# High and low weight parts for two feature pairs at a time, and a shorter bank-by-bank end

## The chip, the cores and the metric

The kernel runs on one core of one Trainium2 chip. The metric is the device time of one execution in microseconds (us). TensorE (PE) multiplies, VectorE (DVE), ScalarE (ACT) and GpSimd (POOL) work on elements, and SyncE (SP) issues most of the transfers.

## The reference

One layer of a hybrid block over 512 tokens and 2048 features, in float32:

```python
h = rmsnorm(x, norm1_w[l])
proj = jnp.einsum('bsd,de->bse', h, w_in[l])          # 2048 -> 22592 columns
q, k, v, g_ret, z, xbc, dt_raw, gate_r, gate_s = jnp.split(proj, offsets, axis=-1)
y_r = retention(q, k, v, positions) * silu(g_ret)     # 8 heads x 256
y_s = ssd(xbc, dt_raw, conv_w[l], ...)                # 64 heads x 64
y_s = rmsnorm(y_s * silu(z), ssd_norm_w[l])
p_r = jnp.einsum('bse,ed->bsd', y_r, w_br_ret[l])     # 2048 x 2048
p_s = jnp.einsum('bse,ed->bsd', y_s, w_br_ssd[l])     # 4096 x 2048
merged = sigmoid(gate_r) * p_r + sigmoid(gate_s) * p_s
x = x + jnp.einsum('bsd,de->bse', merged, w_out[l])   # 2048 x 2048
return rmsnorm(x, norm_f_w)
```

Nearly all of the work is the five products with weights. The rest, retention and the state-space scan, is done between them.

## The kernel before

**Tiling.** Every product with weights is cut into units of 256 output columns by 512 tokens over 2048 features. The features of a unit are taken in eight feature pairs (`NP`), each 256 rows of the weights. A unit either uses seven products per feature pair (`SEVEN`, Strassen's products in Winograd's form, four PSUM banks, on seven weight forms of 128 columns) or eight plain ones (`EIGHT`, three banks, four weight forms). The trace holds 101 units of the first kind; the others, and the two passes of the last unit, are plain.

**Parts.** A float32 operand is split into a high part, rounded to the type that TensorE takes at speed, and a low part, which is the remainder. ACT copies to the high part and DVE subtracts (`split`, lines 150 and 151). Each product is then three matmuls: weight high by activation high (line 202), weight high by activation low (line 203), weight low by activation high (line 204). `hh` and `hl` are the parts of the activations, eight tiles of each for a whole stage; `whi` and `wlo` are those of the weights.

**The weight pipeline** (`products`). For every two feature pairs one tile `wf` is loaded by SP (line 216) and three DVE instructions form the combined weights for both at once (lines 219, 221, 222). Then, for each feature pair by itself, `split` makes a `whi` and a `wlo` of 7 x 128 columns (4 x 128 in a plain unit). There are `FB` = 3 tiles `wf`, `HB` = 7 tiles `whi` and `LB` = 6 tiles `wlo`. The tile `wf` is free again when both of its splits are done; a `whi` or `wlo` is free when the last matmul that reads it is done.

**The end of a unit.** The first `NP - LAST` = 5 feature pairs are multiplied one after the other into all banks. The last three are multiplied bank by bank, so that the first banks are complete before the unit ends and can be read out (lines 256 to 260, 250 to 253 in a plain unit) while the others are still being filled. In the retention and scan stages every unit has the same four banks `pb`; in the branch and output stages the banks alternate between `pb` and a second set, `att`.

**Order.** Each engine runs its instructions in one fixed order, which a planner lays down when the program is built, from its own costs, with a head start (`PRIO`) for the weight pipeline and with priority for a unit's read-out. An instruction that waits holds up everything behind it on its engine.

**Stages in time.** Loading and normalising x (to about 75 us), retention (to about 840), the scan with the gates (to about 1860), three branch projections with 2048 features each, then the output projection. Before each branch projection and the output one `load_operands` brings eight feature pairs of activations, POOL and DVE combine them (lines 155 to 160), ACT and DVE split them (lines 150 and 151 again, into `hh` and `hl`; in the first stage all of these show as line 120, the helper that keeps the order of the text).

Of the kernel before, what the change touches and what calls it, by code (L numbers as in the profile page):

```python
# [9 lines left out]
F32R = mybir.dt.float32r  # L10
# [3 lines left out]
PSUM = bass.MemoryType.PSUM  # L14
DRAM = bass.MemoryType.DRAM

P = 128
T = 512
TB = T // P
D = 2048  # L20
# [11 lines left out]

# columns of the constant array
C_ID, C_TRI, C_ONE, C_FREQ, C_END = 0, 128, 256, 384, 386


def _parts_of_inverse_two_pi():
    """1/(2 pi) as a sum of 12-bit pieces, high to low."""
    digits = 0.15915494309189533576888376337251436203445964574045644874766734405889
    from fractions import Fraction  # L40

    # 1/(2 pi) to 200 bits by Machin's formula
    def atan_inv(n, bits):
        one = 1 << bits
        term = one // n
        total, k, sign = term, 1, 1
        while term:
            term //= n * n
            k += 2
            sign = -sign  # L50
            total += sign * (term // k)
        return total

    bits = 240
    pi = 4 * (4 * atan_inv(5, bits) - atan_inv(239, bits))
    inv = Fraction(1 << bits, 2 * pi)
    assert abs(float(inv) - digits) < 1e-15
    parts = []
    for i in range(5):
        step = Fraction(1, 1 << (14 + 12 * i))  # L60
        n = inv // step
        parts.append(float(n * step))
        inv -= n * step
    return parts


def constants():
# [7 lines left out]
    for h in range(NH):  # L75
# [5 lines left out]

# A 256-row by 256-column block of weights B times a 256-feature by 512-token block of
# activations A.  Rows of A are the token halves, its columns the two feature tiles; t1 is
# half 1 and t0 is half 2, the odd weight tile is column 1 and the even one column 2.
# Activation slots: 0 A21, then A12-(A21+A22-A11), 1 A11, 2 A22, 3 A12, 4 A21+A22,
# 5 A21+A22-A11, 6 A21-A11.
# Weight slots: 0 B12, then B22+B11-B12, 1 B11, 2 B22, 3 B21, 4 B11-B12, 5 B22-B12,
# 6 B21-(B22+B11-B12).
# A product is (bank, half of the bank, weight slot, activation slot).
# SEVEN: Strassen's products in Winograd's form.  EIGHT: the block product with A21 as  # L90
# A11+(A21-A11), on the weights as they are.
SEVEN = (((0, 0, 1, 1), (1, 0, 3, 3), (1, 1, 0, 5)),
# [4 lines left out]
         ((2, 0, 0, 6), (2, 0, 2, 2), (2, 1, 2, 3)))  # L97
# EIGHT in two passes, the second half of the tokens first, each with banks of its own.
PASSES = ((((0, 0, 1, 1), (0, 1, 0, 1)), ((1, 0, 3, 3), (1, 1, 2, 3))),
          (((2, 0, 1, 6), (2, 0, 3, 2), (2, 1, 0, 6), (2, 1, 2, 2)),))  # L100
NP = KD // 2
LAST = 3
FB, HB, LB = 3, 7, 6
FORM_POOL = (1, 2, 3, 4, 5, 6, 7)
# [7 lines left out]
class InOrder:  # L112
    """An engine whose instructions issue in the order of the program."""

# [15 lines left out]
def hybrid_block(tc, A, out):  # L130
# [18 lines left out]
    def split(dst_hi, dst_lo, src):  # L149
        ACT.copy(dst_hi, src)  # L150
        DVE.tensor_tensor(dst_lo, src, dst_hi.bitcast(F32), op=ALU.subtract)  # L151

    # ------------------------------------------------ products with the weights
    def combined(f, eng):
# [7 lines left out]
    def operands(i, f):  # L162
        """The seven activation operands of feature pair i from its raw slots 0-3 in f."""
        combined(f, POOL if i in FORM_POOL else DVE)
        completed(f, DVE)
        hi = hp.tile([P, 7, 256], F32R, name=f"hh{i}", tag=f"hh{i}")
        lo = hp.tile([P, 7, 256], F32R, name=f"hl{i}", tag=f"hl{i}")
        split(hi, lo, f[:, 0:7, :])
        return hi, lo
# [7 lines left out]
    def load_operands(forms, src, last=None):  # L177
        """Operands of 2048 features of a DRAM array [features, T]; the last pair may be on chip."""
        H = []
# [9 lines left out]
    def products(H, parts, pt, groups, PE=PE, after=None):  # L189
        """The products of groups, for 256 columns of weights, into the banks pt: parts are  # L190
        DRAM arrays [2048, n], side by side."""
        started, ws = set(), []
# [14 lines left out]
        for k in range(NP):  # L207
            with tc.high_priority(offset=PRIO):
                if k % 2 == 0:
# [8 lines left out]
                    if not plain:  # L218
# [3 lines left out]
                        DVE.tensor_tensor(f2[:, :, 6, :], f2[:, :, 3, :], f2[:, :, 0, :], op=ALU.subtract)  # L222
                f = f2[:, k % 2]
                hi = wp.tile([P, 7, P], F32R, name="whi", bufs=HB)
                lo = wp.tile([P, 7, P], F32R, name="wlo", bufs=LB)
                split(hi[:, :n, :], lo[:, :n, :], f[:, :n, :])
            ws.append((hi, lo))
            if k < NP - LAST:
# [10 lines left out]
    def unit(H, parts, alt=False, plain=False):  # L239
        """W^T A for 256 columns of weights as two tiles [128, T], feature-major."""  # L240
        nb = 3 if plain else 4
# [21 lines left out]

    # ---------------------------------------------------------------- stage 0
    cc = cst.tile([P, C_END], F32, name="cc")
# [8 lines left out]

    # scratch
    yr_d = dp.tile([D, T], F32, name="yr_d")
# [12 lines left out]
    def inverse_root(dst, ps, y, z, n, DVE=DVE, ACT=ACT):  # L289
        """dst = (ps / n + eps) ** -0.5 for sums in PSUM; a Newton step makes it exact.  # L290
        y, z: room for one tile each."""
        ACT.activation(y, ps, AF.Abs_reciprocal_sqrt, scale=1.0 / n, bias=eps)
# [4 lines left out]

    # forms of the activations before they are split: A8 and B8 serve other ends between
    bg_ctx = ExitStack()
# [15 lines left out]
    with tc.tile_pool(name="st0", bufs=1) as st:  # L315
        def early(tag):
            """Room of an operand that is not yet there."""
            return hp.tile([P, 7 * 256], F32, name=f"e_{tag}", tag=tag)

        # the order of the arithmetic here is that of the text  # L320
        pe, act, dve, pool = (InOrder(tc, e) for e in (PE, ACT, DVE, POOL))
        raw = [early(f"hl{i}")[:, :2 * T].rearrange("p (r t) -> p r t", r=2) for i in range(NP)]
        wdt = early("hh7")[:, :KD * SH].rearrange("p (k c) -> p k c", k=KD)
        for i, x in enumerate(raw):
            SP.dma_start(out=x, in_=rows(A["xT"], i))
            if i == 0:
                SP.dma_start(out=cc, in_=A["consts"])
        # brings the table in ahead
        act.activation(rstd[:, :1], eps, AF.Abs_reciprocal_sqrt)
# [27 lines left out]

        # the normalized activations
        fs, hs, H = {}, {}, []
# [25 lines left out]
    def rotary_tables(positions, x):  # L385
        """cos and sin of the angles, which are rounded as the reference rounds them, then
        counted in turns and reduced exactly; x is room for four tiles."""
        turn, a1, a2, ki = (x[:, i, :] for i in range(4))
# [34 lines left out]
    def step_sizes(v, pool):  # L423
        """dt = softplus(h w + bias), the cumulative decays in blocks of 128 tokens."""
        u, w, s, s2 = (v[:, i, :].rearrange("p (c h) -> p c h", c=TB) for i in range(4))
# [8 lines left out]
        for tb in range(TB):  # L434
            DVE.scalar_tensor_tensor(u[:, tb, :], pt[:, tb * SH:(tb + 1) * SH], rstd[:, tb:tb + 1], dtb,
                                     op0=ALU.mult, op1=ALU.add)
        # softplus: max(u, 0) + log1p(exp(-|u|)), log1p(w) = 2 atanh(w / (2 + w))
        DVE.tensor_scalar(w, u, -1.0, None, op0=ALU.mult)
# [36 lines left out]

    # -------------------------------------------------------------- retention
    with tc.tile_pool(name="ret", bufs=1) as rp:
# [3 lines left out]
        for h in range(NH):  # L481
            # the decays stay where the gate comes later
            dec = sg[:, 0, :]
# [72 lines left out]

    # -------------------------------------------------------------------- SSD
    with tc.tile_pool(name="ssd", bufs=1) as sp:
        # conv taps and bias; D
        cw = sp.tile([P, 48, 5], F32, name="cw")  # L560
# [12 lines left out]
        def conv(x, j, dst):  # L573
            """causal convolution over tokens and SiLU of one feature block."""
            ACT.activation(dst, x, AF.Identity, scale=cw[:, j, 3:4], bias=cw[:, j, 4:5])
# [13 lines left out]
        for g in range(NG):  # L589
# [14 lines left out]
            for jj in range(2):  # L604
# [5 lines left out]
                for e in range(2):  # L610
# [5 lines left out]
                    for i in range(2):  # L616
                        SP.dma_start(out=E[i * 64:(i + 1) * 64, :], in_=E_d[h0 + i, P:].partition_broadcast(64))
                    # x token-major, scaled by dt, and by dt and the decay to the block's end
                    ps = att_tile()
# [21 lines left out]
                    for i in range(2):  # L641
                        # decay from s to l within a block; s > l is zeroed by CB
                        L = sp.tile([P, TB, P], F32, name="L", bufs=2)
# [28 lines left out]

    # --------------------------------------------------- branch projections
    with tc.tile_pool(name="br", bufs=1) as bp:
# [41 lines left out]

    # ----------------------------------------------------- output projection
    with tc.tile_pool(name="fin", bufs=1) as fp:
# [16 lines left out]

        # the last two feature blocks, the odd one first, half of the tokens after the other
        t = xo[NP - 1]
# [85 lines left out]
```

## Time and profile before

| what | value |
|---|---|
| runs | 2796.71, 2796.94, 2799.17 us; median 2796.94 |
| profiled execution, first to last instruction (its span) | 2798.7 us |
| PE / DVE / ACT / POOL busy | 98 / 85 / 48 / 9 % of the span |
| split of weights, ACT high / DVE low | 968 / 968 instructions |
| granted TensorE clock | 0.993 |

The profile gives no time of the profiled execution besides its span, which is 1.8 us above the median of the runs. A change in the span is read as the same change in the time. PE's matmuls overlap, so its busy share counts instructions that follow each other without a gap; short waits show as idle time with the name of what ended them.

### The profile page before, as it was taken

To read this page: it belongs to the slowest core of one execution; us is meant where nothing else is said; L and a number is where in the kernel's file an instruction comes from. 1 tells how busy PE (TensorE), PEld (TensorE's weight loads), DVE (VectorE), ACT (ScalarE), POOL (GpSimd) and SP (SyncE) were. 2 spreads that over 40 slices of the span, in tenths; PEclk is the share of its full clock that TensorE was granted. 3 is DMA by queue.
4 is the path that set the end of the run, shared out by engine and by line. 5 is a ranking of instruction groups with operands and counts; after the bars stand their busy time and mean duration, and the time that the engine had idled before them with its cause. 6 is when DMAs were issued, how large, how long until landed. Compare 5 with 4: busy or idle time off the path is not lost.

```text
span 2798.7 us, 55732 instructions
## 1 busy us (share of the span) xinstructions
PE 2738.8 (98%) x22236; PEld 2680.0 (96%) x22236; DVE 2380.8 (85%) x3746; ACT 1333.9 (48%) x1885; POOL 254.1 (9%) x206
## 2 busy tenths in 40 slices
PE   7999999999999999999999999999999999999898
PEld 4999999999999999999999999999999999999898
DVE  8998888888879888888888888888888798788997
ACT  4434333333345655564655555555553343433443
POOL 4000000000000000000000000000020030111311
PEclk9999999999999999999999999999999999999999
DMA  3333333333333444343443434334455554566634
GB/s 124 106 97 101 102 102 103 110 92 109 102 104 119 127 134 127 108 137 108 127 125 121 135 121 135 104 118 128 124 187 165 167 180 130 166 184 190 220 105 139
DMA packets 344388, 362.69 MB, mean 130 GB/s; under 512 B 25664, under 2 KB 298304, under 8 KB 344128
## 3 DMA queue, kind: packets, MB, share of 16 engines
q1 hardware_dynamic: 323888, 325.32, 38.5%
q10 hardware_dynamic: 20240, 33.82, 3.3%
q8 instruction: 174, 2.85, 0.4%
q14 instruction: 86, 0.70, 0.1%
HBM read 321.56 MB, written 37.49 MB: 128 GB/s over the span
## 4 chain that ended last, share of the span: by engine, by line
PE 82%; DVE 7%; DMA 6%; issue 3%; POOL 1%; ACT 1%; SPq 0%; DVEq 0%; ACTq 0%; POOLq 0%
PE pb L203 22%; PE pb L202 22%; PE pb L204 22%; PE att L204 2%; PE att L202 2%; PE att L203 2%; PE att L651 2%; DVE wlo L151 2%; DMA wf<-in_w_in_dram 2%; PE att L537 1%; PE att L522 1%; DMA wf<-in_w_br_ssd_dram 1%; PE att L655 1%; PE pb L120 1%; PE att L630 1%
## 5 line engine op out<-in xcount | busy, mean ns | idle before, releaser
L203 PE MATMUL pb<-hl,whi 128*128 128x256 f32 x5944 | 1686.5, 285 | 10.8 <-DVE hl L120 6.0
L202 PE MATMUL pb<-hh,whi 128*128 128x256 f32 x5944 | 1685.7, 285 | 6.2 <-ACT hh L150 3.2
L204 PE MATMUL pb<-hh,wlo 128*128 128x256 f32 x5944 | 1673.5, 284 | 3.7 <-DVE wlo L151 3.6
L150 ACT CAST whi<-wf 128x896 fp32r<-128x896 f32 (+1 forms) x968 | 822.1, 885 | 873.9 <-PE pb L203 414.8
L203 PEld LDWEIGHTS pb<-hl,whi 128*128 128x128 f32 x5944 | 1141.9, 192 | 17.6 <-DVE hl L120 6.9
L202 PEld LDWEIGHTS pb<-hh,whi 128*128 128x128 f32 x5944 | 1139.3, 192 | 10.2 <-ACT hh L150 3.6
L204 PEld LDWEIGHTS pb<-hh,wlo 128*128 128x128 f32 x5944 | 1136.0, 192 | 5.5 <-DVE wlo L151 5.1
L151 DVE TENSOR_TENSOR wlo<-wf,whi 128x896 fp32r<-128x896 f32 (+1 forms) x968 | 997.4, 1040 | 78.6 <-PE pb L204 25.9
L219 DVE TENSOR_TENSOR wf<-wf 128x512 f32<-128x512 f32 x404 | 286.3, 709 | 168.1 <-DMA wf<-in_w_in_dram 114.3
L204 PE MATMUL att<-hh,wlo 128*128 128x256 f32 x864 | 241.8, 285 | 7.8 <-DVE wlo L151 7.8
L202 PE MATMUL att<-hh,whi 128*128 128x256 f32 x864 | 245.4, 285 | 1.4 <-ACT whi L150 1.4
L203 PE MATMUL att<-hl,whi 128*128 128x256 f32 x864 | 244.8, 285 | 0.0
L221 DVE TENSOR_TENSOR wf<-wf 128x256 f32<-128x256 f32 x404 | 182.8, 454 | 4.3
L204 PEld LDWEIGHTS att<-hh,wlo 128*128 128x128 f32 x864 | 165.1, 193 | 8.8 <-DVE wlo L151 8.8
L222 DVE TENSOR_TENSOR wf<-wf 128x256 f32<-128x256 f32 x404 | 170.7, 424 | 3.2
L202 PEld LDWEIGHTS att<-hh,whi 128*128 128x128 f32 x864 | 167.6, 194 | 1.8 <-ACT whi L150 1.6
L203 PEld LDWEIGHTS att<-hl,whi 128*128 128x128 f32 x864 | 167.5, 194 | 0.0
L626 POOL TENSOR_TENSOR xl<-xd,sst 128x384 f32<-128x384 f32 x32 | 33.6, 1049 | 876.9 <-DVE xd L623 819.7
L646 ACT ACTIVATE L<-L,sst 128x128 f32<-128x128 f32 x256 | 80.1, 390 | 59.6 <-DMA L<-A_d 47.1
L256 ACT COPY o<-pb 128x256 f32<-128x256 f32 x89 | 32.9, 370 | 144.4 <-PE pb L204 137.2
L257 DVE TENSOR_TENSOR o<-pb,o 128x512 f32<-128x512 f32 x89 | 60.9, 684 | 34.5 <-PE pb L204 34.2
L543 POOL TENSOR_TENSOR rs<-rs,mhalf 128x1 f32<-128x1 f32 x32 | 24.9, 784 | 709.5 <-DVE rs L542 700.2
(230 smaller groups left out, 2113.1 us busy)
## 6 DMA issues: line engine op xcount, KB each, us to landing
wf<-in_w_in_dram SPq DMA_DIRECT2D x640, 256.0 KB, 3.1
wf<-in_w_br_ssd_dram SPq DMA_DIRECT2D x128, 256.0 KB, 3.6
wf<-in_w_out_dram SPq DMA_DIRECT2D x72, 256.0 KB, 3.2
wf<-in_w_in_dram SPq DMA_DIRECT2D x128, 128.0 KB, 2.6
L<-A_d SPq DMA_DIRECT2D x64, 256.0 KB, 3.5
wf<-in_w_br_ret_dram SPq DMA_DIRECT2D x64, 256.0 KB, 3.7
ys_d<-B ACTq DMA_DIRECT2D x32, 256.0 KB, 2.8
E<-E_d SPq DMA_DIRECT2D x64, 96.0 KB, 3.0
```

What stands on the lines that cost most here:

```text
L150: ACT.copy(dst_hi, src)
L151: DVE.tensor_tensor(dst_lo, src, dst_hi.bitcast(F32), op=ALU.subtract)
L202: PE.matmul(o, wh, xh, start=b not in started, stop=False, skip_group_check=True)
L203: PE.matmul(o, wh, xl, start=False, stop=False, skip_group_check=True)
L204: PE.matmul(o, wl, xh, start=False, stop=(k == NP - 1), skip_group_check=True)
L219: DVE.tensor_tensor(f2[:, :, 4:6, :], f2[:, :, 1:3, :], f2[:, :, 0:1, :].to_broadcast([P, 2, 2, P]), op=ALU.subtract)
L221: DVE.tensor_tensor(f2[:, :, 0, :], f2[:, :, 2, :], f2[:, :, 4, :], op=ALU.add)
L222: DVE.tensor_tensor(f2[:, :, 6, :], f2[:, :, 3, :], f2[:, :, 0, :], op=ALU.subtract)
L257: DVE.tensor_tensor(o[:, 1:3, :], pt[1], p1[:, None, :].to_broadcast([P, 2, 256]), op=ALU.add)
L626: POOL.tensor_tensor(xl, xd[:, :TB - 1], tail[:, :TB - 1, hs, None].to_broadcast([P, TB - 1, 2, 64]), op=ALU.mult)
L646: ACT.activation(L[:, c, :], L[:, c, :], AF.Relu, scale=-1.0, bias=At[:, c, h0 + i:h0 + i + 1])
L651: PE.matmul(pi[i * 64:(i + 1) * 64, c * P:(c + 1) * P], xd[:, c, i, :], L[:, c, :], start=True, stop=True)
```

## The change

The high and low parts are formed once for two feature pairs: `whi` and `wlo` become tiles of two, three of each, and `split` covers both pairs in one ACT and one DVE instruction. The bank-by-bank end covers the last two feature pairs where it covered three. (Comment lines are emptied throughout; the line numbers stay.)

```diff
-LAST = 3
-FB, HB, LB = 3, 7, 6
+LAST = 2
+FB, HB, LB = 3, 3, 3
...
                         DVE.tensor_tensor(f2[:, :, 6, :], f2[:, :, 3, :], f2[:, :, 0, :], op=ALU.subtract)
-                f = f2[:, k % 2]
-                hi = wp.tile([P, 7, P], F32R, name="whi", bufs=HB)
-                lo = wp.tile([P, 7, P], F32R, name="wlo", bufs=LB)
-                split(hi[:, :n, :], lo[:, :n, :], f[:, :n, :])
-            ws.append((hi, lo))
+
+                    hi = wp.tile([P, 2, 7, P], F32R, name="whi", bufs=HB)
+                    lo = wp.tile([P, 2, 7, P], F32R, name="wlo", bufs=LB)
+                    split(hi[:, :, :n, :], lo[:, :, :n, :], f2[:, :, :n, :])
+            ws.append((hi[:, k % 2], lo[:, k % 2]))
```

**The end of a unit on PE.** The fourth unit of the first state-space branch projection, banks `att`; `hh5` to `hh7` are the feature pairs 5 to 7. The place is the step from the second bank to the third. Before:

```order
L202 MATMUL att_27195<-hh7_26473,whi_27355 128x256
L203 MATMUL att_27195<-hl7_26474,whi_27355 128x256
L204 MATMUL att_27195<-hh7_26473,wlo_27356 128x256
L202 MATMUL att_27196<-hh5_26453,whi_27341 128x256
L203 MATMUL att_27196<-hl5_26454,whi_27341 128x256
L204 MATMUL att_27196<-hh5_26453,wlo_27342 128x256
```

The same step in the changed kernel, on PE:

```order
L202 MATMUL att_25611<-hh7_24937,whi_25776 128x256
L203 MATMUL att_25611<-hl7_24938,whi_25776 128x256
L204 MATMUL att_25611<-hh7_24937,wlo_25777 128x256
L202 MATMUL att_25612<-hh6_24927,whi_25776 128x256
L203 MATMUL att_25612<-hl6_24928,whi_25776 128x256
L204 MATMUL att_25612<-hh6_24927,wlo_25777 128x256
```

The third bank is resumed at feature pair 6 where it was resumed at 5, and pairs 6 and 7 read the same tiles `whi_25776` and `wlo_25777`.

**The read-out of that unit on DVE.** The four rows with `o` are the read-out; `wf` and `wlo` are the next units' weights. Before:

```order
L257 TENSOR_TENSOR o_27422<-att_27195,o_27422 128x512
L222 TENSOR_TENSOR wf_27581<-wf_27581 128x2x128
L258 TENSOR_TENSOR o_27422<-o_27422,att_27196 128x2x256
L151 TENSOR_TENSOR wlo_27522<-wf_27490,whi_27521 128x896
L259 TENSOR_TENSOR o_27422<-o_27422,att_27196 128x256
L151 TENSOR_TENSOR wlo_27553<-wf_27546,whi_27552 128x896
L260 TENSOR_TENSOR o_27422<-att_27197,o_27422 128x2x256
```

The same read-out in the changed kernel:

```order
L257 TENSOR_TENSOR o_25822<-att_25611,o_25822 128x512
L221 TENSOR_TENSOR wf_25990<-wf_25990 128x2x128
L258 TENSOR_TENSOR o_25822<-o_25822,att_25612 128x2x256
L222 TENSOR_TENSOR wf_25990<-wf_25990 128x2x128
L259 TENSOR_TENSOR o_25822<-o_25822,att_25612 128x256
L151 TENSOR_TENSOR wlo_25945<-wf_25938,whi_25944 128x1792
L219 TENSOR_TENSOR wf_26054<-wf_26054 128x2x256
L260 TENSOR_TENSOR o_25822<-att_25613,o_25822 128x2x256
```

Two low parts of 896 columns stood inside the read-out, and now one of 1792 does, behind the last reading of the third bank.

**The first activations on DVE.** In the first stage `A8`, `B8`, `C7` are activations on their way to `hh` and `hl`, and `e_hl` the normalised x. From the low part of feature pair 4 to that of pair 6, before:

```order
L120 TENSOR_TENSOR hl4_273<-B8_246,hh4_255 128x1792
L120 TENSOR_TENSOR A8_268<-A8_268 128x256
L151 TENSOR_TENSOR wlo_465<-wf_457,whi_464 128x512
L120 TENSOR_TENSOR A8_268<-A8_268 128x256
L120 TENSOR_TENSOR B8_279<-e_hl7_115,R1_81 128x512
L120 TENSOR_TENSOR hl5_284<-C7_257,hh5_266 128x1792
L151 TENSOR_TENSOR wlo_606<-wf_599,whi_605 128x896
L120 TENSOR_TENSOR B8_279<-B8_279 128x256
L219 TENSOR_TENSOR wf_711<-wf_711 128x2x256
L151 TENSOR_TENSOR wlo_631<-wf_599,whi_630 128x896
L120 TENSOR_TENSOR B8_279<-B8_279 128x256
L120 TENSOR_TENSOR hl6_290<-A8_268,hh6_277 128x1792
```

The same stretch in the changed kernel:

```order
L120 TENSOR_TENSOR hl4_273<-B8_246,hh4_255 128x1792
L120 TENSOR_TENSOR A8_268<-A8_268 128x256
L151 TENSOR_TENSOR wlo_473<-wf_469,whi_472 128x2x512
L120 TENSOR_TENSOR A8_268<-A8_268 128x256
L120 TENSOR_TENSOR B8_279<-e_hl7_115,R1_81 128x512
L120 TENSOR_TENSOR hl5_284<-C7_257,hh5_266 128x1792
L120 TENSOR_TENSOR B8_279<-B8_279 128x256
L219 TENSOR_TENSOR wf_687<-wf_687 128x2x256
L120 TENSOR_TENSOR B8_279<-B8_279 128x256
L120 TENSOR_TENSOR hl6_290<-A8_268,hh6_277 128x1792
```

The first unit's last low parts now stand in one place behind `hl4` (one of them stood ahead of it), and the two low parts of the next unit that stood between `hl5` and `hl6` have moved behind `hl6`.

## The prediction

> **What bounds the kernel now.** I read the page's busy shares first, then the timeline of PE in a quiet place, the stretches, PE's waits, and last the engines that feed it.
>
> ```profile
> span 2798.7 us, 55732 instructions
> ...
> PE 2738.8 (98%) x22236; PEld 2680.0 (96%) x22236; DVE 2380.8 (85%) x3746; ACT 1333.9 (48%) x1885; POOL 254.1 (9%) x206
> ```
>
> PE has 59.9 us without an instruction in the whole span. A busy share can still hide a slow pace, so the next view is a piece of the timeline (start, duration, engine, operation).
>
> ```profile
> 1000.18 0.28 PE L204 MATMUL pb<-hh,wlo 128*128 128x256 f32 x1
> 1000.30 0.28 PE L202 MATMUL pb<-hh,whi 128*128 128x256 f32 x1
> 1000.42 0.28 PE L203 MATMUL pb<-hl,whi 128*128 128x256 f32 x1
> ```
>
> A matmul starts every 0.12 us. The change neither removes nor adds a matmul, so it can only act on the gaps. One feature pair of a `SEVEN` unit is 21 matmuls, 2.52 us of PE. Where the gaps lie is told by stretches (length, then busy time of PE, PEld, DVE, ACT, POOL, then clock and DMA):
>
> ```profile
> 8.00:75.00 67.00, 53.49 (x243) 33.35 (x243) 63.28 (x82) 30.85 (x32) 29.94 (x20) 0.90 0.37 116
> 840.00:1860.00 1020.00, 1019.24 (x8504) 1006.98 (x8503) 871.35 (x1382) 577.05 (x905) 63.36 (x51) 1.00 0.41 123
> 2480.00:2560.00 80.00, 74.24 (x590) 73.27 (x589) 71.48 (x106) 24.26 (x30) 17.07 (x9) 0.96 0.60 185
> 2560.00:2640.00 80.00, 69.69 (x558) 68.67 (x558) 69.41 (x92) 33.85 (x38) 23.88 (x18) 0.96 0.62 193
> ```
>
> The scan is full: 0.8 us of gap in 1020. The gaps lie in the first 75 us and where activations are loaded anew; between 2480 and 2640 there are 16.1 us, with DVE busy for 140.9 of the 160. PE's own waits name the same places (what was waited for, us in total, times, longest), first over the span, then from 90 to 1860 us alone, where these three rows are all there are:
>
> ```profile
> PE att L204 <- DVE wlo L151: 7.8, 5, 3.3
> PE pb L203 <- DVE hl L120: 6.0, 4, 3.0
> PE pb L203 <- DVE hl L151: 4.7, 2, 4.5
> PE pb L204 <- DVE wlo L151: 3.6, 5, 1.1
> PE pb L202 <- ACT hh L150: 3.2, 2, 2.9
> ...
> PE att L595 <- ACT A L580: 2.0, 1, 2.0
> PE pb L202 <- DVE o L259: 0.4, 1, 0.4
> PE att L651 <- DVE L L649: 0.4, 1, 0.4
> ```
>
> The first five sum to 25.3 us, 0.9% of the span. That is all that a faster DVE or ACT can give back: 6.0 in the first stage, 19.3 at the later ones. (The waits for x and its norm, ahead of the first product with weights, are left out.)
>
> **The fewer instructions.** 968 ACT copies and 968 DVE subtractions become 484 each. The groups (count, then busy us, mean ns) price them; `hl` is the same subtraction at the new size, 1792 columns, and `hh` the same copy.
>
> ```profile
> L151 DVE TENSOR_TENSOR wlo<-wf,whi 128x896 fp32r<-128x896 f32 x808 | 880.6, 1098 | 56.7 <-ACT whi L150 20.6 <-PE pb L204 19.9 <-ACT L L646 7.4
> L151 DVE TENSOR_TENSOR wlo<-wf,whi 128x512 fp32r<-128x512 f32 x160 | 117.5, 746 | 22.0 <-issue 10.9 <-PE pb L204 6.0 <-PE att L204 2.2
> L151 DVE TENSOR_TENSOR hl<-B,hh 128x1792 fp32r<-128x1792 f32 x12 | 25.2, 2101 | 1.4 <-ACT hh L150 1.4
> L150 ACT CAST whi<-wf 128x896 fp32r<-128x896 f32 x808 | 725.7, 938 | 759.0 <-PE pb L203 338.7 <-DVE wf L222 291.8 <-issue 37.0
> L150 ACT CAST hh<-B 128x1792 fp32r<-128x1792 f32 x12 | 20.3, 1693 | 17.6 <-DVE B L160 14.2 <-DVE f L711 3.4
> ```
>
> By durations one DVE instruction of 2.10 takes the place of two of 1.098: 0.10 saved. Durations overlap a little, so I also take the distance to the next start:
>
> ```profile
> 2342.32 1.08 DVE L151 TENSOR_TENSOR wlo<-wf,whi 128x896 fp32r<-128x896 f32 x1
> 2343.33 0.41 DVE L259 TENSOR_TENSOR o<-o,att 128x256 f32<-128x256 f32 x1
> ...
> 2622.69 2.01 DVE L151 TENSOR_TENSOR hl<-A,hh 128x1792 fp32r<-128x1792 f32 x1
> 2624.63 0.41 DVE L221 TENSOR_TENSOR wf<-wf 128x256 f32<-128x256 f32 x1
> ```
>
> 1.01 for the small one, 1.94 for the large: 2.02 - 1.94 = 0.08 saved a pair. With 404 pairs of the 896 form and 80 of the 512 form that is about 484 x 0.08 = 39 us off DVE's 2380.8, 1.6%. ACT saves 2 x 0.938 - 1.693 = 0.18 a pair, some 87 us of 1333.9. None of it is on PE's path while PE does not wait, so in the scan and in retention I put its worth at nothing; the cover there is the ready weights, reckoned next.
>
> **The cover.** Weights are made ahead, as far as buffers are free. Before, the tail of a unit holds feature pairs 5, 6 and 7 to its last bank; the low part of pair 5 is released four products, 12 matmuls, 1.44 us, ahead of the end, and its buffer serves pair 3 of the next unit, which PE needs 3 x 2.52 = 7.56 us after the end. Of these 9.0 us the split takes 0.94 + 1.10 = 2.04, which leaves 7.0 us, the narrowest place; elsewhere it is five pairs, 12.6 - 2.04 = 10.6. After, a tile of two is released every 5.04 us and needed two tiles, 10.08 us, later; its split takes 1.69 + 2.10 = 3.79, which leaves 6.3 us for the even pair and 8.8 for the odd. So the narrowest place loses 0.7 us and a usual one 1.8 to 4.3. Is so much in use? The engines' own waits say how often the buffers are the limit:
>
> ```profile
> ACT whi L150 <- PE pb L203: 414.8, 192, 5.7
> ...
> DVE wlo L151 <- PE pb L204: 25.9, 40, 2.0
> ...
> SPq L216 <- DVE wlo L151: 1101.5, 300, 11.3
> ```
>
> DVE found its buffer still in use 40 times in 968, ACT 192 times: DVE runs after its work, and seldom after a free buffer, and SP waits for DVE to release a `wf`. A loss of buffers that are seldom all full costs nothing by itself. Bounds for the middle of the kernel: 0, and 1.2 us (half of the time by which a pair's even part comes later: 0.75 on ACT and 0.93 on DVE, with a little lost on the way) at each of the some ten places where the cover is used up, 12 us. I take 0, because PE waited 2.8 us in 1770 there and not once for a weight.
>
> **The shorter tail.** The second bank is complete 4 x 2 x 3 x 0.12 = 2.88 us ahead of the unit's end where it was 4.32, the third 1.44 where it was 2.16. The next unit writes the third bank 1.08 us after the end, so its readings (lines 258 and 259) have 2.52 us where they had 3.24:
>
> ```profile
> L258 DVE TENSOR_TENSOR o<-o,pb 128x512 f32<-128x512 f32 x89 | 60.7, 682 | 29.8 <-PE pb L204 29.2
> L259 DVE TENSOR_TENSOR o<-o,pb 128x256 f32<-128x256 f32 x89 | 36.6, 412 | 0.0
> ```
>
> They take 1.09 us, or 3.03 with a low part of 1.94 between them. In the planned order that stands so in 24 of these 89 units (a low part of 1.01 in 77 before). Where it does, 0.5 us may show, if the planner had no time to spare; its price is between 0 and 24 x 0.5 = 12 us. I take 0: before, with low parts between them in 77 units, PE waited for line 259 0.4 us in the scan.
>
> **The first stage.** Here PE waits for `hl`, and DVE's order moves. DVE's timeline shows what stood ahead of the low parts:
>
> ```profile
> 53.62 0.94 DVE L120 TENSOR_TENSOR C<-C 128x256 f32<-128x256 f32 x1 [0.56 <-POOL C L120]
> 54.49 1.78 DVE L151 TENSOR_TENSOR wlo<-wf,whi 128x512 fp32r<-128x512 f32 x1
> ...
> 60.62 1.76 DVE L151 TENSOR_TENSOR wlo<-wf,whi 128x512 fp32r<-128x512 f32 x1
> ...
> 65.18 1.62 DVE L151 TENSOR_TENSOR wlo<-wf,whi 128x896 fp32r<-128x896 f32 x1
> ...
> 69.54 2.01 DVE L120 TENSOR_TENSOR hl<-A,hh 128x1792 fp32r<-128x1792 f32 x1
> ```
>
> Two of three low parts ahead of `hl6` are gone or merged into the second, and the pieces at 54.49 and 65.18 no longer stand ahead of it. But DVE waits for POOL as well (0.56 us at 53.62), so what goes is partly filled by that wait: the rounds with a low part were 6.1 us (54.49 to 60.62), and POOL still has to be waited for. Bounds: 0, and the 6.0 us that PE waited. I take 1.5, nearer the lower end because of the 0.56.
>
> These low parts took 1.78 us where their group's mean is 0.746. The Trainium skill ("SBUF — State Buffer", section "Who interferes with whom") says that a DVE instruction with both inputs in SBUF and a GpSimd instruction that reads SBUF block each other entirely, the later one behind the earlier. The stretched row fits that; by that rule the pair's instruction would be held once rather than twice, and would hold POOL for longer, and the sum above does not use it.
>
> **The later loads.** In the 160 us from 2480 there are some 32 pairs, 32 x 0.08 = 2.6 us less for DVE, of which PE may see as much as it waits for DVE: I take 1.5 off. Against it, where PE already waits for a `wlo` (10 times), a pair is ready later than its even half was, by 0.93 us; half of the ten at that price is 4.7, and with other matmuls set ahead by the planner I take 1.5 on. Net 0, between -12 (most of the 19.3) and +14 (below).
>
> **The sum.** 0 (scan and retention) + 0 (tail) - 1.5 (first stage) + 0 (later loads) = -1.5 us on the profiled 2798.7. The same step from the median of 2796.94 is 2795.4.
>
> **The rivals.** *DVE is the real limit at every load.* Then 1.6% of DVE, the better order of the first stage and ACT's 87 us pay where PE waits: half of the 25.3 us, 12.6, gives 2784. For it: DVE is at 88% in the stretches that lose most, and PE waits there for DVE's results. Against: much of the waiting is for a chain through POOL and transfers, which are not shortened.
>
> *The pair is ready too late.* A feature pair's weights used to come one by one; now the even one waits for the odd one, 0.75 us on ACT and 0.93 on DVE, 1.7 together. Where the ready weights run out, PE pays it. The point from which it decides is a cover below 1.7 us: the 17 waits for `wlo`, `hl` and `hh` outside the scan are such places, and half of them at 1.7 is 14 us, 2811. For it: with DVE at 85% and not full, the saved overhead is worth little and the delay is real. Against: the narrowest cover falls only from 7.0 to 6.3. The Trainium skill ("Perfetto Trace Analysis", section "Optimizing Scalar/DVE Operations") has this rule: if ScalarE or VectorE is not saturated but leaves other engines waiting, smaller instructions may finish what is needed sooner, and grouping pays where the engine is saturated. By that rule this change is on the wrong side in most of the kernel; the waits in this trace, which are at DVE's fullest places, leave it open.
>
> *The read-out collides.* If line 259 comes late in the 24 units, the next unit's third bank is held: 12 us, 2809.
>
> **How the numbers follow.** A difference under 0.2%, 5.6 us, cannot be told from no change here. My forecast has 0.42, with its own range 2789 to 2801, and 0.03 of that lies below the 0.2%. DVE as the limit has 0.30, the late pair 0.20, the colliding read-out 0.08. So faster 0.33, same 0.39, slower 0.28. The range runs from the first rival's value to a little short of the last ones': 2784 to 2809.
>
> **What would show it.** The groups should show 404 low parts of 1792 columns near 2.05 us, DVE near 2340 busy, ACT near 1250, and PE's waits for `hl` in the first stage below 6.0. I am wrong to the slow side if waits of PE for `wlo` or for `o` appear between 90 and 1860 us, and to the fast side if the 16.1 us of gaps from 2480 to 2640 shrink by more than half.

## The result, and the profile after

The changed kernel takes 2869.21 us (2863.76 to 2873.40) where the kernel before took 2796.82: 1.0254 times as long, 95% interval 1.0238 to 1.027. It is slower by 72 us, far outside the range. The profiled execution spans 2871.3 us, 72.6 more than before. Its page:

```profile
span 2871.3 us, 54169 instructions
...
PE 2762.7 (96%) x22236; PEld 2695.8 (94%) x22236; DVE 2338.2 (81%) x3262; ACT 1296.5 (45%) x1415; POOL 279.4 (10%) x206
```

DVE has 43 us less to do, as forecast, and PE's gaps have grown from 59.9 to 108.6 us. PE's busy time has grown as well, by 23.9 us for the same 22236 matmuls. The groups of the new instructions (busy us, mean ns, idle time before them and what ended it):

```profile
L150 ACT CAST whi<-wf 128x1792 fp32r<-128x1792 f32 x404 | 681.4, 1691 | 846.2 <-PE pb L203 437.7 <-DVE wf L222 197.3 <-issue 60.1
L151 DVE TENSOR_TENSOR wlo<-wf,whi 128x1792 fp32r<-128x1792 f32 x404 | 820.1, 2032 | 131.6 <-ACT whi L150 131.2
```

The prices are close to those of the prediction. Most of the time is lost in the scan. (The scan does not end at about 1860 us, as said of the kernel before: there the last Exp of a head, L648, starts at 2049.6 us, and the first weights of a branch projection are loaded at 2059.9.) Its stretch, from the first convolution to the first read-out of a branch projection, is 57 us longer; first before, then after (length, busy PE, PEld, DVE, ACT, POOL, clock, DMA):

```profile
809.00:2124.00 1315.00, 1308.55 (x10891) 1291.93 (x10891) 1119.68 (x1760) 739.01 (x1146) 97.81 (x81) 1.00 0.42 127
```

```profile
815.00:2187.00 1372.00, 1321.34 (x10803) 1296.41 (x10802) 1087.97 (x1528) 731.62 (x935) 127.08 (x81) 0.99 0.40 121
```

The other 15.6 us are 6 ahead of this stretch and 9.6 behind it. In the scan PE stood still for 6.4 us before and for 50.7 now. The four longest waits there are these, after; before, L256 had none, and the other three had these small rows:

```profile
PE att L651 <- DVE L L649: 0.4, 1, 0.4
PE pb L204 <- DVE wlo L151: 0.2, 1, 0.2
PE pb L202 <- DVE o L257: 1.0, 1, 1.0
```

And after:

```profile
PE att L651 <- DVE L L649: 15.8, 15, 3.0
PE pb L204 <- DVE wlo L151: 9.7, 16, 1.5
PE pb L202 <- DVE o L257: 9.2, 8, 1.3
PE pb L202 <- ACT o L256: 7.2, 5, 3.4
```

Only one of the four rows is a wait for weights. The others wait for the heads' decays (L649) and for the read-out of banks (256, 257): for work that shares DVE and ACT with the splits. Over the whole span DVE now waits longer for ACT's high parts, and ACT for the transfer of L, a head's decays; before, then after:

```profile
DVE wlo L151 <- ACT whi L150: 20.6, 29, 1.3
ACT L L646 <- DMA L<-A_d: 47.1, 33, 4.0
```

```profile
DVE wlo L151 <- ACT whi L150: 174.6, 131, 6.1
ACT L L646 <- DMA L<-A_d: 80.1, 28, 6.7
```

A half group is half of one of the scan's eight groups of heads. The timeline of a first half group of the changed kernel (rows of SP, DVE, ACT and PE; the first number is the start) shows how one delay is handed on:

```profile
1372.65 0.90 SPq L216 DMA_DIRECT2D wf<-in_w_in_dram  x2
1373.66 0.40 SPq L644 DMA_DIRECT2D L<-A_d  x1
...
1370.60 2.03 DVE L151 TENSOR_TENSOR wlo<-wf,whi 128x1792 fp32r<-128x1792 f32 x1 [0.88 <-ACT whi L150]
...
1377.98 1.28 ACT L646 ACTIVATE L<-L,sst 128x128 f32<-128x128 f32 x4 [3.99 <-DMA L<-A_d]
1379.16 1.67 ACT L150 CAST whi<-wf 128x1792 fp32r<-128x1792 f32 x1
...
1381.71 2.02 DVE L151 TENSOR_TENSOR wlo<-wf,whi 128x1792 fp32r<-128x1792 f32 x1
...
1385.05 0.69 DVE L257 TENSOR_TENSOR o<-pb,o 128x512 f32<-128x512 f32 x1
...
1383.78 0.39 PE L204 MATMUL pb<-hh,wlo 128*128 128x256 f32 x1 [0.62 <-DVE wlo L151]
1385.79 0.48 PE L202 MATMUL pb<-hh,whi 128*128 128x256 f32 x1 [1.27 <-DVE o L257]
```

A low part ends at 1372.63 and sets its `wf` free; only then does SP load the next `wf`, and L stands behind that on SP. ACT stands still 3.99 us for L, with the next high part behind it; the low part of that pair comes at 1381.71, and PE waits for it, and then for line 257, which is behind it on DVE.

The wait costs more than its length. Here are 3.48 us of PE ahead of it and the 3.48 us behind it (the clock is the last number but two):

```profile
1376.00:1379.48 3.48, 3.48 (x32) 3.48 (x31) 3.06 (x7) 1.50 (x5) 0.00 (x0) 1.00 0.79 268
1385.79:1389.27 3.48, 3.48 (x17) 3.48 (x18) 3.48 (x5) 1.55 (x3) 1.20 (x1) 0.52 0.49 154
```

Behind the wait the granted clock is 0.52, and the row counts 17 matmuls where the other counts 32. The trace's record of the granted clock has nine such stretches at half clock in the scan after, 34 us in all, and one of 3.4 us before. So of the scan's 57 us 44 are gaps, and the other 13 are a longer busy time of PE, for which 31 us more at half pace are enough. What decides which wait is followed by such a stretch was not tested.

In this plan the order of ACT has changed too. In seven second half groups the first Exp (L648) stands ahead of the Silu of z (L609), and the function's table is loaded twice more each time, 14 loads of 1.28 us. The half group of the timeline is none of them: its Silu of z, at 1360.53 us, stands ahead of its first Exp.

### The profile page after: what moved, and what is told of

It reads as the page before. It is cut to its first block, busy times and chain, and to the rows that moved or that the text cites. A ratio compares the mean times of both kernels' runs of the same rounds, so it can differ in the third digit from the quotient of the medians.

```text
span 2871.3 us, 54169 instructions
## 1 busy us (share of the span) xinstructions
PE 2762.7 (96%) x22236; PEld 2695.8 (94%) x22236; DVE 2338.2 (81%) x3262; ACT 1296.5 (45%) x1415; POOL 279.4 (10%) x206
## 5 line engine op out<-in xcount | busy, mean ns | idle before, releaser
L204 PE MATMUL pb<-hh,wlo 128*128 128x256 f32 x5944 | 1666.4, 286 | 18.2 <-DVE wlo L151 17.8
L150 ACT CAST whi<-wf 128x1792 fp32r<-128x1792 f32 (+1 forms) x484 | 765.2, 1584 | 997.8 <-PE pb L203 556.3
L204 PEld LDWEIGHTS pb<-hh,wlo 128*128 128x128 f32 x5944 | 1134.5, 193 | 25.8 <-DVE wlo L151 24.1
L151 DVE TENSOR_TENSOR wlo<-wf,whi 128x1792 fp32r<-128x1792 f32 (+1 forms) x484 | 920.0, 1904 | 175.2 <-ACT whi L150 174.6
L646 ACT ACTIVATE L<-L,sst 128x128 f32<-128x128 f32 x256 | 80.3, 390 | 97.7 <-DMA L<-A_d 80.1
L665 POOL TENSOR_TENSOR R<-R,B 128x512 f32<-128x512 f32 x31 | 76.2, 2457 | 316.5 <-ACT B L664 316.5
L649 DVE TENSOR_TENSOR L<-L,A 128x512 f32<-128x512 f32 x64 | 51.1, 809 | 57.3 <-ACT L L648 57.3
```

The source lines that it names most:

```text
L204: PE.matmul(o, wl, xh, start=False, stop=(k == NP - 1), skip_group_check=True)
L646: ACT.activation(L[:, c, :], L[:, c, :], AF.Relu, scale=-1.0, bias=At[:, c, h0 + i:h0 + i + 1])
L649: DVE.tensor_tensor(L, L, CB, op=ALU.mult)
L665: POOL.tensor_tensor(sq, sq, sz[e], op=ALU.add)
```

## The experiments

The planner lays each kernel out anew, so an edit also changes the order. The times, in us, and the time that DVE waited for ACT's high part:

| run | parts | LAST | us | ratio to before, interval | DVE for ACT |
|---|---|---|---|---|---|
| before | one by one | 3 | 2796.8 | 1 | 20.6 |
| after | pairs | 2 | 2869.2 | 1.0254 (1.0238-1.027) | 174.6 |
| e1 | tiles of two, one by one | 2 | 2812.5 | 1.0059 (1.0044-1.0075) | 87.5 |
| e2 | one by one | 2 | 2792.8 | 0.9989 (0.9979-0.9998) | 7.0 |
| e3 | pairs | 3 | 2835.3 | 1.0142 (1.0125-1.0159) | 88.0 |
| e4 | one by one, six high tiles | 3 | 2803.1 | 1.0023 (1.0014-1.0033) | 75.0 |
| e5 | pair on ACT alone | 2 | 2862.3 | 1.0238 (1.0223-1.0254) | 153.0 |
| e6 | pair on DVE alone | 2 | 2837.3 | 1.0154 (1.0139-1.0169) | 181.8 |
| e7 | pairs, Exp behind Silu | 2 | 2804.2 | 1.0029 (1.0018-1.004) | 143.8 |
| e8 | one by one, Exp behind Silu | 3 | 2801.6 | 1.0017 (1.0007-1.0026) | 6.9 |
| e9 | one by one, Exp first | 3 | 2797.3 | 1.0009 (0.9999-1.0018) | 19.9 |
| e10 | pair on DVE alone, Exp behind Silu | 2 | 2813.7 | 1.0064 (1.0047-1.0081) | 153.3 |
| e11 | pairs, Exp behind Silu | 3 | 2809.5 | 1.0049 (1.0034-1.0064) | 61.2 |
| e12 | one by one | 1 | 2838.9 | 1.0152 (1.0137-1.0167) | 13.2 |
| e13 | pairs, Exp first | 2 | 2836.0 | 1.0148 (1.0127-1.0169) | 163.8 |
| e14 | pairs, three tiles L | 2 | 2832.9 | 1.0135 (1.0117-1.0153) | 192.8 |
| e15 | tiles of two, one by one, Exp behind Silu | 2 | 2822.1 | 1.01 (1.0077-1.0122) | 69.7 |
| e16 | as e2, five rounds | 2 | 2793.1 | 0.999 (0.9981-1.0) | 8.3 |

Each ratio goes by runs of the kernel before that were taken with that kernel. The differences in us below are between the medians of the table, if no ratio is named; the two ways differ by up to 3 us.

**Size, tail, cover.** e1 splits the changed kernel's instructions again, e2 and e4 change one number of the kernel before, e3 one of the changed kernel.

```diff
-split(hi[:, :, :n, :], lo[:, :, :n, :], f2[:, :, :n, :])          # e1
+for m in range(2):
+    split(hi[:, m, :n, :], lo[:, m, :n, :], f2[:, m, :n, :])
-LAST = 3                                                          # e2, of before
+LAST = 2
-LAST = 2                                                          # e3, of after
+LAST = 3
-FB, HB, LB = 3, 7, 6                                              # e4, of before
+FB, HB, LB = 3, 6, 6
```

> The changed kernel, but each split is again two ACT and two DVE instructions, one for each feature pair, into the tiles of two (three of each, LAST 2). Theory 'cover' (tiles are given back two at a time, and only three of them): the loss stays, 2855 to 2880. Theory 'instruction size' (a pair's instruction comes late and stands for 2 us in front of other work on ACT and DVE): most of the 72 us come back, 2795 to 2815.

> The kernel before with LAST 2 alone. Theory 'tail' (the shorter bank-by-bank end leaves the read-out 1.44 us less, and PE waits for line 257): slower by 12 to 30 us, 2809 to 2827, with waits of PE for line 257 or 256 in the scan. Theories 'cover' and 'instruction size': no loss, 2790 to 2800, since weight buffers come free sooner.

> The changed kernel with LAST 3, pairs and buffers as changed. Theory 'tail': the eight waits of 1.43 us for line 257 go, 2840 to 2860. Theory 'cover': with LAST 3 two of the three tiles are held to the end of the unit and one is ready for the next, so it is slower still, 2890 to 3000. Theory 'instruction size': about as the changed kernel, 2860 to 2880.

> The kernel before with six high tiles where it had seven, so that it holds as many bytes of parts as the changed one. Theory 'cover': slower, 2803 to 2820. Theories 'instruction size' and 'tail': no change, 2794 to 2800.

With small instructions into the same tiles 57 of the 72 us are gone, and 15.7 stay. The Trainium skill ("Perfetto Trace Analysis", section "Optimizing Scalar/DVE Operations") says that smaller instructions may finish work sooner where an engine is not saturated but holds others up; e1 agrees, with 57 us, though e15 below does not. The shorter tail alone costs nothing: e2 gains 3 us by its ratio. With pairs, though, LAST 3 is 34 us better than LAST 2, below what each of the three theories gave, and not worse as 'cover' had it. One high tile less costs 6 us, at the lower end of what 'cover' gave. No theory had all four right.

**Which engine.** e5 and e6 keep one of the two long instructions.

```diff
-split(hi[:, :, :n, :], lo[:, :, :n, :], f2[:, :, :n, :])
+ACT.copy(hi[:, :, :n, :], f2[:, :, :n, :])                        # e5; e6 the other way round
+for m in range(2):
+    DVE.tensor_tensor(lo[:, m, :n, :], f2[:, m, :n, :], hi[:, m, :n, :].bitcast(F32), op=ALU.subtract)
```

> The changed kernel with one ACT copy for a pair, but two DVE subtractions, one for each feature pair. Theory 'ACT size' (the pair's copy on ACT, and the order of ACT that the planner makes with it, is the loss): 2845 to 2885, with 25 loads of the table ahead of line 650, the Exp. Theory 'DVE size' (a subtraction of 2 us is in the way on DVE): 2805 to 2825, near the kernel with tiles alone.

> The changed kernel with one DVE subtraction for a pair, but two ACT copies. Theory 'ACT size': 2800 to 2825, near the kernel with tiles alone. Theory 'DVE size': 2845 to 2885.

Either one alone loses: 65.5 us with the long copy, 40.5 with the long subtraction. e5 came out as 'ACT size' has it, with 25 table loads ahead of the Exp where the kernel before has 17; e6 has 17, and its time lies between the two theories. So table loads are not needed for a loss.

**The order.** e7 adds one rule for the planner to the changed kernel, e8 the same rule to the kernel before. It only fixes what is issued first; no wait for data is added.

```diff
-ACT.activation(sz[e], x, AF.Silu)
+zi = ACT.activation(sz[e], x, AF.Silu).ins.name
...
-ACT.activation(L, L, AF.Exp, scale=-1.0)
+le = ACT.activation(L, L, AF.Exp, scale=-1.0).ins
+tc.add_manual_dep(le, zi, ..., reason="order of issue")
```

> The changed kernel with one more rule for the planner: the Exp of a head (line 648) is issued behind the Silu of z of its half group (line 609), as it stands in the order of the kernel before. Theory 'ACT order' (the loss of the scan is the planned order with 14 more table loads on ACT): 25 to 55 us come back, 2815 to 2845, and PE's waits for line 649 go. Theory 'size alone' (the long instructions delay whatever stands behind them in any order): 2860 to 2875.

> The control: the same rule for the planner on the kernel before, where the Exp stands behind the Silu already in nearly all places. Both theories: 2788 to 2802. If it is much faster or slower, the rule does more than undo the extra table loads, and the run beside it cannot be read.

The rule gives back 65 us, more than expected, and leaves 8 over the kernel before by the ratio. On the kernel before it costs 5 us by the ratio. The scan of e7, and all of PE's waits over 0.5 us in it:

```profile
812.00:2130.00 1318.00, 1309.73 (x10893) 1292.96 (x10892) 1093.75 (x1542) 713.79 (x921) 127.61 (x81) 1.00 0.41 128
```

```profile
PE pb L203 <- DVE hl L151: 4.5, 2, 3.7
PE pb L202 <- ACT hh L150: 1.4, 1, 1.4
PE pb L202 <- ACT o L250: 1.1, 1, 1.1
PE pb L202 <- DVE o L252: 0.7, 2, 0.5
```

The scan is 1318 us again, with the same long instructions in the same tiles, and the waits for decays and for line 256 are gone; of the wait for line 257 0.2 us is left. DVE still waits 143.8 us for ACT here: that wait alone is not the loss.

**The order without pairs, and with them.** e9 forces the early Exp on the kernel before, e13 the same lines on the changed one: the first L of a second half group is made ahead of z's unit, its Exp behind the Silu of x, and the Silu of z behind that.

> The kernel before, with the order of ACT that the changed kernel has in the scan forced on it: in each second half group the first Exp is issued behind the Silu of x and ahead of the Silu of z, with 16 more table loads. Theory 'ACT order': slower by 25 to 60 us, 2820 to 2855, with waits of PE for line 257 or 256 and the product with the Exp in it. Theory 'pairs needed' (such an order only hurts with instructions of two pairs): within 12 us, 2790 to 2808.

> The changed kernel with the Exp forced ahead of the Silu of z in every second half group, by the same lines that cost the kernel before 3 us (16 extra table loads). Theory 'order times long instructions': 2850 to 2890, as the changed kernel. Theory 'something else in the planned order': 2800 to 2830.

With single parts the early Exp and its 16 table loads cost 3 us, with an interval that holds 1. With pairs the same lines cost 32 us against e7. e13 fell between what the two theories gave: this detail of the order hurts only with the pairs, but it is only half of the 65 us. Together with e10 and e11, the rule on two kernels that have no extra table loads without it:

> Two ACT copies and one DVE subtraction for a pair, with the Exp behind the Silu of z. That kernel without the rule took 2837 us and had no extra table loads. Theory 'any order the planner makes in the scan': the rule makes another order and most of it comes back, 2795 to 2815. Theory 'table loads alone': nothing comes back, 2830 to 2842.

> The changed kernel with LAST 3 and the Exp behind the Silu of z. With LAST 3 and without the rule it took 2835 us and had no extra table loads. Theory 'cover' (two of three tiles of two are held to the end of a unit): 2825 to 2845, slower than the same with LAST 2 (2804). Theory 'order only': 2798 to 2810, as with LAST 2.

Both got more than half of their loss back, 23.6 us and 25.8, though there were no extra table loads to take away. So another order of the same instructions is worth that much; which part of it, these two do not tell. With the rule LAST 2 and LAST 3 differ by 5 us.

**A link, and a counterexample.** e14 gives L a third tile (`bufs=3`), so that its transfer can start sooner; its order keeps the early Exp, with 25 and 7 table loads at lines 648 and 609 (24 and 7 in the changed kernel). e15 is e1 with the rule.

> The changed kernel with three tiles L where it had two, so that the transfers of L can start earlier; the extra table loads stay in its order (25 and 7). Theory 'ACT stands still behind the transfer of L' (80 us of waits): 2810 to 2840, with that wait below 40 us. Theory 'the order by itself': 2855 to 2880.

> Tiles of two with an instruction for each feature pair, LAST 2, and the Exp behind the Silu. Without the rule 2812 us. Theory 'order': 2795 to 2804. Theory 'cover' (tiles given back in twos): 2808 to 2816.

e14 gave back 36 us, half. Rows of it:

```profile
ACT L L646 <- DMA L<-A_d: 47.1, 19, 3.2
...
PE pb L204 <- DVE wlo L151: 20.0, 34, 1.8
...
PE pb L202 <- DVE o L257: 0.2, 1, 0.2
```

ACT's wait for L fell from 80.1 to 47.1, what it is in the kernel before, though the expectation was below 40. PE's wait for line 257 fell from 9.2 to 0.2 and its wait for L649 is gone, while the waits for `wlo` stayed (17.8 in the changed kernel). So the transfer of L is one link of the chain, as the timeline suggests, though the other parts of the order moved a little too. e15 missed on both theories: the rule that saves the pairs makes e1 slower by 9.6 us. PE waits 19.0 us there for POOL's `xl` (line 626 of the changed kernel), from which the state of a head is made. The rule is no remedy by itself: it gave three better plans (e7, e10, e11) and two worse ones (e8, e15).

**A faster one?** e12 shortens the tail further, e16 repeats e2 in five rounds.

> The kernel before with LAST 1, a candidate for a faster one. If the read-out has time to spare: 2788 to 2796, as with LAST 2 (2792.8). If not: PE waits for lines 257 to 259 at each unit's end, 2810 to 2850.

> The kernel before with LAST 2 once more, in five rounds. If the shorter tail is a gain: 0.9975 to 0.9995 of the kernel before, with an interval below 1. If not: an interval that holds 1.

```profile
PE pb L202 <- ACT o L256: 27.5, 15, 3.3
```

LAST 1 leaves the read-out too little time: PE waits 27.5 us for line 256, where lines 257 to 259 were expected. LAST 2 with single parts is the fastest kernel of all, by 0.1%, and its interval in e16 reaches 1.

## Why the prediction was wrong

- **The failed step is "The cover": "I take 0, because PE waited 2.8 us in 1770 there and not once for a weight".** The scan lost 57 us. That PE did not wait before says that the cover sufficed, not how much of it was left. I reckoned the cover for PE's use of weights alone, 7.0 against 6.3 us. But ACT and DVE also carry the heads and the read-out, in one fixed order, and there the long instructions stand in front of them: three of PE's four longest waits in the scan are for the heads and the read-out, 32.2 us, and one for weights, 9.7. The cover did shrink: DVE's wait for ACT's high parts goes from 20.6 us to 75.0 with one high tile less (e4), and to 174.6 with pairs. But that alone is not the loss. In e7 DVE still waits 143.8 us, and ACT waits for its buffers as before the rule (565.1 us, and 556.3 in the changed kernel), with 8 us lost.
- **I took the planned order as given.** I compared it at three places, none in the scan's ACT, where the first Exp had moved. e7 shows that another order of the same instructions is worth 65 of the 72 us. One detail of the order, the early Exp, costs 3 us on single parts (e9) and 32 on pairs (e13). Neither alone is the cause: pairs in the good order cost 8 us, pairs in the planner's own 72. The planner's whole order was not tried on single parts.
- **"It can only act on the gaps" was wrong.** No matmul was added, yet PE's busy time grew by 23.9 us, 12.8 of them in the scan, where the clock is halved behind some of the new waits.
- **The tail** was rightly put at 0 by itself (e2). That it is not 0 together with pairs (34 us in e3) follows from no step of mine; with the rule it turns round, and LAST 2 is 5 us better than LAST 3.
- **The instructions** were sized well on DVE, 2.03 us for the pair and 2338 busy for some 2340. ACT saved 57 us in its group (822.1 to 765.2) and not 87. Its busy time counts the overlap of copies once: 808 times 0.938 is 758 us, where the row of before has 725.7. ACT as a whole is at 1296.5 where I had said 1250; 18 us of it are the 14 table loads.
- **The first stage** gave none of the 1.5 us: PE's waits for `hl` there went from 6.0 to 7.9 us.
- **The rivals.** "The pair is ready too late" had the right sign and named the delay of 1.7 us, but put it at the loads of activations and at 14 us. "The read-out collides" had the right sign too, but at another line: PE waited 0.6 us for line 259 in the scan, 9.2 for 257 and 7.2 for 256. DVE as the limit did not show: it had 43 us less to do, and behind the scan, where the loads are, the time grew by 9.6 us.

What stays open: which part of the planner's order costs what. Early Exp (e13) and L's transfer (e14) each account for about half, and may overlap; e6 and e15 lose 40 and 25 us with neither extra load nor early Exp, by plans that were not taken apart. Every edit and every rule makes the planner lay out the whole kernel anew, so no run changes one place of the order alone. More pair tiles, which would test the cover by itself, were not tried.

## What to carry to other kernels

An engine at 85% with PE at 98% is not a reason to save its instructions: ask first how deep the buffers let the engines run ahead, and whether a longer instruction stands in front of other work in their fixed orders. Before an instruction is made larger in a kernel with a planner, compare the whole order of every engine that carries it, above all which waits now stand ahead of it; an early Exp that was harmless with short instructions (3 us) cost 32 with long ones. A wait that is absent says nothing of the room that is left; take one buffer away to see it (6 us for one of seven here).

## What the runs showed of the hardware

Sixteen more loads of ACT's function table, 1.28 us each or 20.5 together, cost the kernel before about 3 us (e9, 5 at the end of its interval), with ACT 48% busy. Behind a wait of PE the granted clock was halved for some 3.4 us (0.52 from 1385.79 to 1389.27 us), nine times in the scan of the changed kernel and once in that of the kernel before. And 43 us less of DVE's work, in a kernel that had DVE 85% busy, did not make it faster in any order that was tried: the best one is 8 us slower.
